# The end of a one-core decoder layer: combining additions of the first row tile ahead of the second's, small sums of squares joined or moved to ScalarE

## The chip, the core and the metric

The kernel runs on one core of a Trainium2 chip. The core has TensorE for matmuls (its results go to PSUM, in banks of 128 x 512 float32), VectorE and ScalarE for elementwise work, GpSimd, and SyncE, which mostly issues DMAs; each works through its own queue of instructions in order and waits on semaphores for the others. SBUF is the working memory of 128 partitions. The metric is the device time of one execution in microseconds, the median of several runs. In the profile's rows PE is TensorE, PEld its weight load, DVE VectorE, ACT ScalarE, POOL GpSimd, SP SyncE; a small q behind a name is that engine's sequencer.

## What is computed

One decoder layer on 256 tokens of width 2048: a normalized input goes through sparse attention and a convolution module side by side, then a gated MLP with a short causal convolution, then a last RMS norm. The change touches only the last line: the residual sum and that norm.

```python
def rms_norm(x, g):
    xf = x.astype(jnp.float32)
    y = xf * lax.rsqrt(jnp.mean(xf * xf, axis=-1, keepdims=True) + NORM_EPS)
    return (y * g.astype(jnp.float32)).astype(x.dtype)
...
        x = x + jnp.concatenate([attn, conv], axis=-1) @ w_out[l]
        h = rms_norm(x, ffn_norm_g[l])
        x = x + conv_glu_ffn(h, w_up[l], ffn_conv_w[l], ffn_conv_b[l], w_down[l])
    return rms_norm(x, final_norm_g)
```

## The kernel before

The 256 tokens are two row tiles of 128 tokens (`t` = 0 and 1), each on the 128 partitions; `x2[:, t]` holds a row tile's 2048 columns of the residual sum, and the tail below adds the MLP's result into it and norms it. Every float32 product is made of three or four matmuls of a high and a low part (`wh`, `wl`, `gh`, `gl`).

The MLP's down projection runs in two halves of 1024 output columns (`h`), 22 chunks of weights each. Many chunks are of the kind "S": a scheme with 7 products in place of 8, whose results stand in banks by name (1 to 8) and have to be combined by additions at the end. In the second half, name 2 is bank 6 and name 3 is bank 7 (row tile 0, its two quarters of 512 columns), name 4 is bank 0 and name 8 is bank 1 (row tile 1); names 1, 5, 6 and 7 are banks 2, 3, 4 and 5. `combine` (L1409) returns the nine steps: ScalarE copies bank 2 to `c`; bank 3 is added to the second quarter of row tile 0 (step 1) and of row tile 1 (step 2); `u` = bank 4 + `c` (step 3); `v` = `u` - bank 5 (step 4); row tile 0 gets + `c` (step 5) and - `u` (step 6); row tile 1 gets + `v` (step 7) and - `v` (step 8).

The last two chunks are of kind "D", plain products, and `last_quad` (L1476) puts them out in six pieces, so that the norm can begin early: for each row tile its third quarter (columns 1024 to 1536) whole, piece 0, in banks 6 and 0, and its last quarter (1536 to 2048) as two pieces of 256 columns, in banks 2 and 4 for row tile 0 and banks 3 and 5 for row tile 1. Those four banks are free only when `combine` has read them.

`last_add` (L1447) adds a piece to `x2` on VectorE; ScalarE squares and sums it into a column of `ss3`. Columns 0 and 1 of `ss3` were filled long before, from the first 1024 columns. `last_root` (L1454) sums the squares of the last piece on VectorE (the custom instruction), starting from the sum of the others, and GpSimd raises it to the power -0.5: the root `r`. `last_scale` (L1465) multiplies by the root, ScalarE for columns of the first half (already multiplied by the weights of the norm) and VectorE for the second half with the weights, and issues the store. The small sums that join the columns of `ss3` are instructions of 128 x 1: `mean_of` (L275) on VectorE, `more` (L1481) on ScalarE.

The order on each engine is the order of the code (the schedule is manual): all of `combine` for both row tiles, then the direct additions of banks 7 and 1 (L1518), then row tile 0's pieces, its small sums and root, then row tile 1. SyncE issues the stores, ScalarE the very last one.

Of the kernel before, what the change touches and what calls it, by code (L numbers as in the profile page):

```python
# [11 lines left out]
F32 = mybir.dt.float32  # L12
F32R = mybir.dt.float32r
AF = mybir.ActivationFunctionType
# [39 lines left out]
def hybrid_trunk(ctx: ExitStack, tc: tile.TileContext, a: dict, out: bass.AP):  # L54
# [220 lines left out]
    def mean_of(pool, parts_, count, acc=EPS):  # L275

        for p_ in parts_:
            ms = pool.tile([P, 1], F32, name="ms", bufs=4)
            nc.vector.tensor_scalar(ms, p_, 1.0 / count, acc, op0=OP.mult, op1=OP.add)
            acc = ms  # L280
        return acc
# [925 lines left out]
    with ExitStack() as fx:  # L1207
# [239 lines left out]
        def last_add(b, t, i):  # L1447
            lo, hi = LAST[i]
            xq = x2[:, t, 1024 + lo:1024 + hi]
            nc.vector.tensor_add(xq, b, xq)  # L1450
            if i < 2:
                nc.scalar.activation(sq3[:, :hi - lo], xq, AF.Square, scale=ROOT, accum_out=ss3[:, t, 2 + i:3 + i])

        def last_root(t, acc):  # L1454
            lo, hi = LAST[2]
            xq = x2[:, t, 1024 + lo:1024 + hi]
            nc.vector.tensor_tensor_reduce(out=sq3[:, 256:], in0=xq, in1=xq, scale=1.0 / D, scalar=acc,
                                           op0=OP.mult, op1=OP.add, accum_out=ss3[:, t, 4:5])
            r = fw.tile([P, 1], F32, name="rstd", bufs=2)
            nc.gpsimd.tensor_tensor(r, ss3[:, t, 4:5], half, op=OP.pow)  # L1460
            return r

        accs = []

        def last_scale(t, r3, lo, hi, whole=True, between=None, queue=nc.sync):  # L1465
            there, here = [v.rearrange("p (a c) -> p a c", a=2)[:, :, lo:hi] for v in (out_rows[:, t], x2[:, t])]
            nc.vector.scalar_tensor_tensor(here[:, 1], here[:, 1], r3, gfin[:, 1024 + lo:1024 + hi],
                                           op0=OP.mult, op1=OP.mult)
            if not whole:
                nc.sync.dma_start(there[:, 1], here[:, 1])  # L1470
                there, here = there[:, :1], here[:, :1]
                accs.append(between())
            nc.scalar.activation(x2[:, t, lo:hi], x2[:, t, lo:hi], AF.Copy, scale=r3)
            queue.dma_start(there, here)

        def last_quad(ws2, g, b0):  # L1476

            def sums(t, parts_, acc=EPS):
                return mean_of(fw, [ss3[:, t, i:i + 1] for i in parts_], 1, acc)

            def more(t, i, acc):  # L1481
                new = fw.tile([P, 1], F32, name="more", bufs=2)
                nc.scalar.activation(new, ss3[:, t, i:i + 1], AF.Identity, bias=acc)
                return new

            for i in range(3):
                last_add(last_products(ws2, g, b0[0], 0, i), 0, i)
            acc = sums(1, range(2))
            r0 = last_root(0, sums(0, range(4)))
            b = last_products(ws2, g, b0[1], 1, 0)  # L1490
            nc.vector.tensor_add(x2[:, 1, 1024:1536], b, x2[:, 1, 1024:1536])
            last_scale(0, r0, 0, 512)
            nc.scalar.activation(sq3, x2[:, 1, 1024:1536], AF.Square, scale=ROOT, accum_out=ss3[:, 1, 2:3])
            last_add(last_products(ws2, g, b0[1], 1, 1), 1, 1)
            last_scale(0, r0, 512, 1024, False, lambda: more(1, 3, sums(1, (2,), acc)))
            last_add(last_products(ws2, g, b0[1], 1, 2), 1, 2)
            r1 = last_root(1, accs.pop())
            for lo, hi in ((0, 256), (256, 512), (512, 1024)):
                last_scale(1, r1, lo, hi, queue=nc.scalar if hi == 1024 else nc.sync)

# [10 lines left out]
        for h in range(2):  # L1511
            nb = dict(zip((2, 3, 4, 8, 1, 5, 6, 7), ring[4 * h:] + ring[:4 * h]))
            for q in range(NQ):
                g = gq.pop(0)
                if h == 1 and q == NQ - 1:
                    run_todo(99)
                    for t in range(2):
                        nc.vector.tensor_add(x2[:, t, 1536:], nb[names[t, 1]], x2[:, t, 1536:])  # L1518
                    ws2 = w_next(), w_next()
                    last_quad(ws2, g, [nb[names[t, 0]] for t in range(2)])  # L1520
                    break
                if prev and q == 0:
                    todo.extend(lambda t=t, n=n, nb=prev: first_add(nb, t, n) for t in range(2) for n in range(2))
                    todo.extend(lambda i=i: first_half(i // 2, i % 2) for i in range(4))
                for j in range(2):
                    p = 2 * q + j
                    down_pair(h, p, g, j, nb)
                    if KINDS[h].rfind("S") == p:
                        todo.extend(combine(h, nb))
            prev = nb  # L1530

# [97 lines left out]
```

## Time and profile before

| what | value |
|---|---|
| median of 3 runs | 1082.1 us (1082.0 to 1082.76) |
| the profiled execution | 1081.91 us |
| its span, first to last instruction | 1080.1 us |
| granted TensorE clock, mean | 0.998 of full |
| TensorE busy | 1070.4 us, 99% of the span |
| VectorE busy | 897.6 us, 83% |
| ScalarE busy | 619.9 us, 57% |
| GpSimd busy | 367.8 us, 34% |
| 1060 to 1066 us: VectorE / ScalarE busy | 5.95 / 0.00 of 6 us |
| 1066 to 1070 us: VectorE / ScalarE busy | 3.60 / 1.27 of 4 us |
| 1070 to 1075 us: TensorE / VectorE / ScalarE busy | 1.93 / 4.06 / 4.03 of 5 us |

The span is 1.8 us shorter than the run's own time, which also has what lies around the first and the last instruction. Times in rows are microseconds from the start of the span. A timeline row is start, duration, engine, line of the code, operation, out<-in, the shape and how many; where several of one line follow each other they are merged (x2, x3) into one duration. What stands in brackets behind a row is how long the engine was idle ahead of it, and what ended that.

### The profile page before, as it was taken

The page shows a single profiled execution, that of the slowest core. Times are in us where ns is not written, and L with a number is a line of the kernel's source. Part 1 is how long each engine was busy: PE and PEld are TensorE (multiplying, and loading weights), DVE is VectorE, ACT ScalarE, POOL GpSimd, SP SyncE. Part 2 cuts the span into 40 slices and gives each one's busy share as a digit, 9 for nine tenths or more (in the row PEclk, how much of TensorE's full clock was granted, in tenths as well). Part 3 has the DMA queues.
Part 4 walks back from the last instruction along what each step waited for, and adds up shares of the span by engine and source line. Part 5 has one row for each costly group of instructions (what it writes and reads, how often), then busy time and mean ns, then how long its engine had stood idle before and what let it go on. Part 6 is the DMA issues. An engine that isn't in the chain of part 4 may idle for free.

```text
span 1080.1 us, 17521 instructions
## 1 busy us (share of the span) xinstructions
PE 1070.4 (99%) x6721; PEld 954.3 (88%) x6721; DVE 897.6 (83%) x1429; ACT 619.9 (57%) x895; POOL 367.8 (34%) x420
## 2 busy tenths in 40 slices
PE   9999999999999999999999999999999999999996
PEld 9999999998788888888888888888888888888886
DVE  6799976777896677878787888878788899999997
ACT  7544456878755555556555555555555556565563
POOL 0888966657100202324233433212121222211220
PEclk9999999999999999999999999999999999999999
DMA  9776757323555878999999999866667699979982
GB/s 353 245 259 257 210 150 240 119 79 118 195 195 199 273 237 244 287 289 282 296 267 304 294 295 299 280 224 224 225 216 276 208 393 352 344 286 345 336 311 98
DMA packets 62016, 272.82 MB, mean 253 GB/s; under 512 B 8187, under 2 KB 11531, under 8 KB 42348
## 3 DMA queue, kind: packets, MB, share of 16 engines
q1 hardware_dynamic: 34748, 199.33, 51.4%
q0 software_dynamic: 23536, 65.29, 22.7%
q10 hardware_dynamic: 3648, 7.08, 1.9%
q8 instruction: 53, 0.87, 0.3%
q14 instruction: 31, 0.25, 0.1%
HBM read 254.87 MB, written 41.18 MB: 274 GB/s over the span
## 4 chain that ended last, share of the span: by engine, by line
PE 96%; DVE 2%; ACT 1%; issue 0%; POOLq 0%; POOL 0%; DVEq 0%; ACTq 0%
PE bank L1355 30%; PE bank L1357 15%; PE bank L253 6%; PE bank L255 6%; PE bank L244 5%; PE bank L246 5%; PE bank L245 5%; PE bank L256 3%; PE bank L254 3%; PE bank L261 3%; PE bank L262 3%; PE bank L263 3%; PE bank L1009 1%; PE bank L986 1%; PE bank L941 1%; DVE wl L211 1%
## 5 line engine op out<-in xcount | busy, mean ns | idle before, releaser
L1355 PE MATMUL bank<-xt,wh 128*128 128x512 f32 x1408 | 488.6, 394 | 0.0
L206 ACT ACTIVATE wh<-wraw 128x1024 fp32r<-128x1024 f32 (+2 forms) x187 | 263.4, 1430 | 279.9 <-issue 113.1
L1357 PE MATMUL bank<-xt,wl 128*128 128x256 f32 x1408 | 390.1, 277 | 0.0
L211 DVE TENSOR_TENSOR wl<-wraw,wh 128x2048 fp32r<-128x2048 f32 (+1 forms) x133 | 254.6, 1919 | 104.9 <-ACT wh L206 104.9
L1355 PEld LDWEIGHTS bank<-xt,wh 128*128 128x128 f32 x1408 | 264.0, 188 | 61.3
L1357 PEld LDWEIGHTS bank<-xt,wl 128*128 128x128 f32 x1408 | 264.2, 188 | 0.0
L244 PE MATMUL bank<-xt,wh 128*128 128x256 f32 x502 | 143.7, 286 | 0.0
L246 PE MATMUL bank<-xt,wl 128*128 128x256 f32 x502 | 142.1, 283 | 0.0
L245 PE MATMUL bank<-xt,wh 128*128 128x256 f32 x502 | 142.0, 283 | 0.0
L211 POOL TENSOR_TENSOR wl<-wraw,wh 128x1024 fp32r<-128x1024 f32 (+1 forms) x54 | 122.6, 2325 | 18.7 <-ACT wh L206 18.7
L128 DVE TENSOR_TENSOR wl<-wraw,wh 128x2048 fp32r<-128x2048 f32 x44 | 100.4, 2285 | 4.6 <-ACT wh L127 4.5
L244 PEld LDWEIGHTS bank<-xt,wh 128*128 128x128 f32 x502 | 96.1, 192 | 1.5 <-issue 0.9
L245 PEld LDWEIGHTS bank<-xt,wh 128*128 128x128 f32 x502 | 96.2, 192 | 0.4
L246 PEld LDWEIGHTS bank<-xt,wl 128*128 128x128 f32 x502 | 96.2, 192 | 0.1
L518 DVE SCALAR_TENSOR_TENSOR bank<-us,cw,bank 128x256 f32<-128x256 f32 x232 | 93.4, 481 | 0.7 <-ACT bank L513 0.3
L1260 POOL DMA_DIRECT2D sum<-in_w_d x84 | 64.5, 846 | 73.2 <-issue 49.2
L127 ACT ACTIVATE wh<-wraw 128x2048 fp32r<-128x2048 f32 x44 | 82.9, 1904 | 7.5 <-PE bank L1355 4.0
L127 ACT ACTIVATE xh<-sums 128x1536 fp32r<-128x1536 f32 x28 | 41.8, 1493 | 78.2 <-DVE sums L156 56.7
L1294 DVE SCALAR_TENSOR_TENSOR yt<-u,fcw,yt 128x255 f32<-128x255 f32 (+1 forms) x176 | 80.9, 480 | 3.1
L1325 POOL DMA_DIRECT2D glf<-glt x22 | 12.9, 586 | 192.3 <-DVE glt L128 136.2
L253 PE MATMUL bank<-wh,gh 128*128 128x512 f32 x167 | 65.6, 393 | 0.0
L255 PE MATMUL bank<-wl,gh 128*128 128x512 f32 x167 | 65.5, 392 | 0.0
(308 smaller groups left out, 1872.0 us busy)
## 6 DMA issues: line engine op xcount, KB each, us to landing
wraw<-in_w_u SPq DMA_DIRECT2D x88, 1024.0 KB, 7.6
wraw<-in_w_t SPq DMA_DIRECT2D x28, 1024.0 KB, 5.1
sum<-in_w_d POOLq DMA_DIRECT2D x84, 256.0 KB, 8.3
wraw<-in_w_d SPq DMA_DIRECT2D x28, 768.0 KB, 7.0
wraw<-in_w_d SPq DMA_DIRECT2D x16, 1024.0 KB, 7.1
gs<-gsf POOLq DMA_DIRECT2D x56, 256.0 KB, 6.3
wraw<-in_w_o SPq DMA_DIRECT2D x13, 1024.0 KB, 4.8
gl<-glf POOLq DMA_DIRECT2D x22, 512.0 KB, 5.4
```

What stands on the lines that cost most here:

```text
L127: nc.scalar.activation(hi, src, AF.Copy)
L128: return lambda: nc.vector.tensor_sub(lo, src, hi.bitcast(F32))
L206: nc.scalar.activation(h[:, sl], raw[:, sl], AF.Copy)
L211: (nc.gpsimd if pooled else nc.vector).tensor_sub(l[:, sl], raw[:, sl], h[:, sl].bitcast(F32))
L244: nc.tensor.matmul(ps, wh, xh, start=first, stop=False)
L245: nc.tensor.matmul(ps, wh, xl, start=False, stop=False)
L246: nc.tensor.matmul(ps, wl, xh, start=False, stop=last)
L253: nc.tensor.matmul(ps, xh, wh, start=first, stop=False)
L255: nc.tensor.matmul(ps, xh, wl, start=False, stop=False)
L518: nc.vector.scalar_tensor_tensor(y[:, j] if last else acc[0], us[:, j, k:k + T], cw[:, j, k:k + 1], acc[0], op0=OP.mult, op1=OP.add)
L1355: nc.tensor.matmul(bk[i], wh[:, k, sl], xt[kt // 4][:, kt % 4].rearrange("p a t -> p (a t)"), start=kt == 0, stop=False)
L1357: nc.tensor.matmul(bk[i][:, :T], wl[:, k, sl], xt_h[kt], start=False, stop=kt == KD - 1)
```

## The change

`last_quad` now receives the nine steps of `combine` and the direct addition as arguments, and places them itself: what row tile 0 needs comes first, row tile 1's additions lie between row tile 0's pieces and behind its sum of squares. Columns 0 and 1 of `ss3` of both row tiles, with the epsilon, are added by one VectorE instruction into `firsts`; the other small sums are made by `more` on ScalarE. In `last_scale` the ScalarE part is written ahead of VectorE's, and where its store is split in two, the half that is stored first is now ScalarE's.

```diff
-        accs = []
...
         def last_scale(t, r3, lo, hi, whole=True, between=None, queue=nc.sync):
             there, here = [v.rearrange("p (a c) -> p a c", a=2)[:, :, lo:hi] for v in (out_rows[:, t], x2[:, t])]
-            nc.vector.scalar_tensor_tensor(here[:, 1], here[:, 1], r3, gfin[:, 1024 + lo:1024 + hi],
-                                           op0=OP.mult, op1=OP.mult)
+            nc.scalar.activation(x2[:, t, lo:hi], x2[:, t, lo:hi], AF.Copy, scale=r3)
             if not whole:
-                nc.sync.dma_start(there[:, 1], here[:, 1])
-                there, here = there[:, :1], here[:, :1]
-                accs.append(between())
-            nc.scalar.activation(x2[:, t, lo:hi], x2[:, t, lo:hi], AF.Copy, scale=r3)
+                nc.sync.dma_start(there[:, 0], here[:, 0])
+                there, here = there[:, 1:], here[:, 1:]
+                between()
+            nc.vector.scalar_tensor_tensor(x2[:, t, 1024 + lo:1024 + hi], x2[:, t, 1024 + lo:1024 + hi], r3,
+                                           gfin[:, 1024 + lo:1024 + hi], op0=OP.mult, op1=OP.mult)
             queue.dma_start(there, here)
...
-            for i in range(3):
-                last_add(last_products(ws2, g, b0[0], 0, i), 0, i)
-            acc = sums(1, range(2))
-            r0 = last_root(0, sums(0, range(4)))
-            b = last_products(ws2, g, b0[1], 1, 0)
-            nc.vector.tensor_add(x2[:, 1, 1024:1536], b, x2[:, 1, 1024:1536])
+            for i in (0, 1, 3, 6):
+                merge[i]()
+            direct(0)
+            merge[5]()
+            firsts = fw.tile([P, 2], F32, name="firsts", bufs=1)
+            nc.vector.scalar_tensor_tensor(firsts, ss3[:, :, 0], EPS, ss3[:, :, 1], op0=OP.add, op1=OP.add)
+            merge[2]()
+            last_add(last_products(ws2, g, b0[0], 0, 0), 0, 0)
+            acc = more(0, 2, firsts[:, :1])
+            merge[4]()
+            last_add(last_products(ws2, g, b0[0], 0, 1), 0, 1)
+            acc = more(0, 3, acc)
+            merge[7]()
+            last_add(last_products(ws2, g, b0[0], 0, 2), 0, 2)
+            r0 = last_root(0, acc)
+            merge[8]()
             last_scale(0, r0, 0, 512)
+
+            def beside():
+                direct(1)
+                b = last_products(ws2, g, b0[1], 1, 0)
+                nc.vector.tensor_add(x2[:, 1, 1024:1536], b, x2[:, 1, 1024:1536])
+
+            last_scale(0, r0, 512, 1024, False, beside)
             nc.scalar.activation(sq3, x2[:, 1, 1024:1536], AF.Square, scale=ROOT, accum_out=ss3[:, 1, 2:3])
+            acc = more(1, 2, firsts[:, 1:])
             last_add(last_products(ws2, g, b0[1], 1, 1), 1, 1)
-            last_scale(0, r0, 512, 1024, False, lambda: more(1, 3, sums(1, (2,), acc)))
+            acc = more(1, 3, acc)
             last_add(last_products(ws2, g, b0[1], 1, 2), 1, 2)
-            r1 = last_root(1, accs.pop())
+            r1 = last_root(1, acc)
...
-                    if KINDS[h].rfind("S") == p:
+                    if h == 0 and KINDS[h].rfind("S") == p:
                         todo.extend(combine(h, nb))
```

TensorE's matmuls keep their number and order. How the other queues change is best seen in the instructions as they stand on each engine (line, operation, out<-in, shape, and what the instruction waits for). The first place is VectorE's queue from its first combining addition to row tile 0's sum of squares; `x2_3709` is the residual sum and `cuv_10666` holds `c`, `u` and `v`. Before:

```order
L1420 TENSOR_TENSOR x2_3709<-bank3_67,x2_3709 128x512 [waits PE_49]
L1420 TENSOR_TENSOR x2_3709<-bank3_67,x2_3709 128x512
L1421 TENSOR_TENSOR cuv_10666<-bank4_68,cuv_10666 128x512 [waits Activation_49]
L1421 TENSOR_TENSOR cuv_10666<-cuv_10666,bank5_69 128x512 [waits DVE_49]
L1422 TENSOR_TENSOR x2_3709<-x2_3709,cuv_10666 128x512 x2
L1423 TENSOR_TENSOR x2_3709<-x2_3709,cuv_10666 128x512 [waits DVE_49]
L1423 TENSOR_TENSOR x2_3709<-x2_3709,cuv_10666 128x512
L1518 TENSOR_TENSOR x2_3709<-bank7_71,x2_3709 128x512 [waits DVE_49]
L1518 TENSOR_TENSOR x2_3709<-bank1_65,x2_3709 128x512 [waits DVE_49]
L1450 TENSOR_TENSOR x2_3709<-bank6_70,x2_3709 128x512 [waits PE_49]
L1450 TENSOR_TENSOR x2_3709<-bank2_66,x2_3709 128x256 [waits DVE_49,PE_49]
L1450 TENSOR_TENSOR x2_3709<-bank4_68,x2_3709 128x256 [waits PE_49]
```

Behind these stood six small sums (L279), then the sum of squares. Of the change, the same place:

```order
L1420 TENSOR_TENSOR x2_3709<-bank3_67,x2_3709 128x512 [waits PE_49]
L1421 TENSOR_TENSOR cuv_10666<-bank4_68,cuv_10666 128x512 [waits Activation_49]
L1422 TENSOR_TENSOR x2_3709<-x2_3709,cuv_10666 128x512 [waits DVE_49]
L1532 TENSOR_TENSOR x2_3709<-bank7_71,x2_3709 128x512 [waits DVE_49]
L1422 TENSOR_TENSOR x2_3709<-x2_3709,cuv_10666 128x512
L1486 SCALAR_TENSOR_TENSOR firsts_10673<-ss3_8766 128x2
L1420 TENSOR_TENSOR x2_3709<-bank3_67,x2_3709 128x512
L1450 TENSOR_TENSOR x2_3709<-bank6_70,x2_3709 128x512 [waits DVE_49,PE_49]
L1421 TENSOR_TENSOR cuv_10666<-cuv_10666,bank5_69 128x512
L1450 TENSOR_TENSOR x2_3709<-bank2_66,x2_3709 128x256 [waits PE_49]
L1423 TENSOR_TENSOR x2_3709<-x2_3709,cuv_10666 128x512 [waits DVE_49]
L1450 TENSOR_TENSOR x2_3709<-bank4_68,x2_3709 128x256 [waits PE_49]
```

Row tile 0's pieces (L1450) moved from rows 10 to 12 to rows 8, 10 and 12, row tile 1's last step (the second L1423, less `v`) and its direct addition (bank 1) moved behind row tile 0's last piece, and the small sums are gone but for `firsts`.

The second place is what follows on VectorE, from row tile 0's sum of squares (L1457) to row tile 1's. Before:

```order
L1457 ISA sq3_8767,ss3_8766<-x2_3709,ms_10732 128x256 [waits DVE_49]
L1457 ISA ss3_8766 128x1
L1491 TENSOR_TENSOR x2_3709<-bank0_64,x2_3709 128x512 [waits PE_49]
L1467 SCALAR_TENSOR_TENSOR x2_3709<-x2_3709,rstd_10735,gfin_4200 128x512 [waits Pool_49]
L1450 TENSOR_TENSOR x2_3709<-bank3_67,x2_3709 128x256 [waits PE_49]
L1467 SCALAR_TENSOR_TENSOR x2_3709<-x2_3709,rstd_10735,gfin_4200 128x512 [waits DVE_49]
L279 TENSOR_SCALAR ms_10773<-ss3_8766,ms_10724 128x1 [waits Activation_49]
L1450 TENSOR_TENSOR x2_3709<-bank5_69,x2_3709 128x256 [waits PE_49]
L1457 ISA sq3_8767,ss3_8766<-x2_3709,more_10775 128x256 [waits DVE_49,Activation_49]
```

Of the change (the second row of both pieces reads the accumulator):

```order
L1457 ISA sq3_8767,ss3_8766<-x2_3709,more_10710 128x256 [waits DVE_49,Activation_49]
L1457 ISA ss3_8766 128x1
L1423 TENSOR_TENSOR x2_3709<-x2_3709,cuv_10666 128x512
L1470 SCALAR_TENSOR_TENSOR x2_3709<-x2_3709,rstd_10727,gfin_4200 128x512 [waits Pool_49]
L1532 TENSOR_TENSOR x2_3709<-bank1_65,x2_3709 128x512 [waits DVE_49]
L1502 TENSOR_TENSOR x2_3709<-bank0_64,x2_3709 128x512 [waits PE_49]
L1470 SCALAR_TENSOR_TENSOR x2_3709<-x2_3709,rstd_10727,gfin_4200 128x512
L1450 TENSOR_TENSOR x2_3709<-bank3_67,x2_3709 128x256 [waits DVE_49,PE_49]
L1450 TENSOR_TENSOR x2_3709<-bank5_69,x2_3709 128x256 [waits PE_49]
L1457 ISA sq3_8767,ss3_8766<-x2_3709,more_10771 128x256 [waits DVE_49,Activation_49]
```

The root runs on GpSimd between the sum of squares and the first scaling (L1467 before, L1470 in the change): beside it VectorE had the addition out of bank 0, and now has the last subtraction of `v`. Both scalings of row tile 0 now stand ahead of row tile 1's second piece (bank 3).

The third place is ScalarE's queue from row tile 0's first square to the last small sum. Before:

```order
L1452 ACTIVATE sq3_8767,ss3_8766<-x2_3709 128x512 [waits DVE_49]
L1452 ACTIVATE sq3_8767,ss3_8766<-x2_3709 128x256 [waits DVE_49,Activation_49]
L1473 ACTIVATE x2_3709<-x2_3709,rstd_10735 128x512 [waits Pool_49]
L1493 ACTIVATE sq3_8767,ss3_8766<-x2_3709 128x512 [waits DVE_49,Activation_49]
L1452 ACTIVATE sq3_8767,ss3_8766<-x2_3709 128x256 [waits DVE_49,Activation_49]
L1483 ACTIVATE more_10775<-ss3_8766,ms_10773 128x1 [waits DVE_49,Activation_49]
```

Of the change:

```order
L1452 ACTIVATE sq3_8767,ss3_8766<-x2_3709 128x512 [waits DVE_49]
L1478 ACTIVATE more_10693<-ss3_8766,firsts_10673 128x1 [waits Activation_49]
L1452 ACTIVATE sq3_8767,ss3_8766<-x2_3709 128x256 [waits DVE_49]
L1478 ACTIVATE more_10710<-ss3_8766,more_10693 128x1 [waits Activation_49]
L1465 ACTIVATE x2_3709<-x2_3709,rstd_10727 128x512 [waits Pool_49]
L1465 ACTIVATE x2_3709<-x2_3709,rstd_10727 128x512
L1505 ACTIVATE sq3_8767,ss3_8766<-x2_3709 128x512 [waits DVE_49]
L1478 ACTIVATE more_10755<-ss3_8766,firsts_10673 128x1 [waits Activation_49]
L1452 ACTIVATE sq3_8767,ss3_8766<-x2_3709 128x256 [waits DVE_49]
L1478 ACTIVATE more_10771<-ss3_8766,more_10755 128x1 [waits Activation_49]
```

Three `more` are added, and the second scaling of row tile 0 moved from behind row tile 1's small sum to ahead of its first square.

More of the change, by code (lines that the diff above doesn't have):

```diff
@@ L1461, in last_root, with last_quad @@
             return r
-        accs = []
         def last_scale(t, r3, lo, hi, whole=True, between=None, queue=nc.sync):
             there, here = [v.rearrange("p (a c) -> p a c", a=2)[:, :, lo:hi] for v in (out_rows[:, t], x2[:, t])]
-            nc.vector.scalar_tensor_tensor(here[:, 1], here[:, 1], r3, gfin[:, 1024 + lo:1024 + hi],
-                                           op0=OP.mult, op1=OP.mult)
+            nc.scalar.activation(x2[:, t, lo:hi], x2[:, t, lo:hi], AF.Copy, scale=r3)
             if not whole:
-                nc.sync.dma_start(there[:, 1], here[:, 1])
-                there, here = there[:, :1], here[:, :1]
-                accs.append(between())
-            nc.scalar.activation(x2[:, t, lo:hi], x2[:, t, lo:hi], AF.Copy, scale=r3)
+                nc.sync.dma_start(there[:, 0], here[:, 0])
[3 more added lines that the diff above has]
+                                           gfin[:, 1024 + lo:1024 + hi], op0=OP.mult, op1=OP.mult)
             queue.dma_start(there, here)
-        def last_quad(ws2, g, b0):
-            def sums(t, parts_, acc=EPS):
-                return mean_of(fw, [ss3[:, t, i:i + 1] for i in parts_], 1, acc)
+        def last_quad(ws2, g, b0, merge, direct):
             def more(t, i, acc):
@@ L1516, in hybrid_trunk @@
                     run_todo(99)
-                    for t in range(2):
-                        nc.vector.tensor_add(x2[:, t, 1536:], nb[names[t, 1]], x2[:, t, 1536:])
                     ws2 = w_next(), w_next()
-                    last_quad(ws2, g, [nb[names[t, 0]] for t in range(2)])
+                    last_quad(ws2, g, [nb[names[t, 0]] for t in range(2)], combine(h, nb),
+                              lambda t: nc.vector.tensor_add(x2[:, t, 1536:], nb[names[t, 1]], x2[:, t, 1536:]))
                     break
```

## Prediction

> **What bounds the kernel now.** I read the chain of waits first, then the timeline of its last 25 us, then the DMA traffic behind the last instruction. On the page the chain is nearly all matmuls, so outside the tail this change has nothing to act on.
>
> ```profile
> PE 96%; DVE 2%; ACT 1%; issue 0%; POOLq 0%; POOL 0%; DVEq 0%; ACTq 0%
> ```
>
> Told in order of time, the tail of that chain seems to run through exactly what is changed: VectorE's additions, the first row tile's root on GpSimd, then the second root.
>
> ```profile
> 1066.15 1.34 DVE x L1450 x3
> ...
> 1069.37 0.56 POOL rstd L1460
> 1069.93 3.14 issue
> ```
>
> The row to stop at is the 3.14 us of "issue": between the two roots the chain shows nothing that was waited for. It went back along GpSimd's own queue to the root before, and GpSimd only stood there. The timeline shows what ended last (start, duration, engine, line, out<-in).
>
> ```profile
> 1071.63 0.21 DVE L279 TENSOR_SCALAR ms<-ss,ms 128x1 f32<-128x1 f32 x1
> 1071.64 0.28 PE L263 MATMUL bank<-wh,gl 128*128 128x256 f32 x1
> ...
> 1071.93 0.29 ACT L1483 ACTIVATE more<-ss,ms 128x1 f32<-128x1 f32 x1
> 1071.96 0.42 DVE L1450 TENSOR_TENSOR x<-bank,x 128x256 f32<-128x256 f32 x1
> ...
> 1072.53 0.48 DVE L1457 CUSTOM_DVE_ANT_0 sq<-x,more 128x256 bf16<-128x256 f32 x1
> ...
> 1073.10 0.55 POOL L1460 TENSOR_TENSOR rstd<-ss,half 128x1 f32<-128x1 f32 x1 [3.18 <-DVE ss L1457]
> 1073.69 1.54 DVE L1467 SCALAR_TENSOR_TENSOR x<-x,rstd,gfin 128x256 f32<-128x256 f32 x3 [0.67 <-POOL rstd L1460]
> 1073.69 1.52 ACT L1473 ACTIVATE x<-x,rstd 128x256 f32<-128x256 f32 x3 [0.86 <-POOL rstd L1460]
> 1075.32 0.64 ACTq L1474 DMA_DIRECT2D out<-x  x1
> ```
>
> The last matmul of the program ends at 1071.64 + 0.28 = 1071.92, and 0.04 later the last addition starts. **That addition waits for TensorE.** From there on everything is serial: addition, sum of squares, root, three scalings, stores. Of the 1080.1 us span, 8.1 lie behind 1071.96. The sum of squares also needs `more` from ScalarE, which was there at 1071.93 + 0.29 = 1072.22, before the addition ended at 1072.38. The wait that stands alone ahead of the sum of squares passed at 1072.4, so the addition was late and `more` was not, with 0.16 us to spare.
>
> ```profile
> L1457 DVEq EVENT_SEMAPHORE  x1: 21/21/21, 1072.4 to 1072.4; - x1
> ```
>
> Last, the stores (stretches; the last two columns are the DMA share and GB/s):
>
> ```profile
> 1075.00:1075.50 0.50, 0.00 (x0) 0.00 (x0) 0.24 (x1) 0.21 (x1) 0.00 (x0) 0.50 0.12 43
> 1075.50:1076.00 0.50, 0.00 (x0) 0.00 (x0) 0.00 (x0) 0.00 (x0) 0.00 (x0) 0.50 1.01 336
> ...
> 1077.50:1078.00 0.50, 0.00 (x0) 0.00 (x0) 0.00 (x0) 0.00 (x0) 0.00 (x0) 0.50 1.03 385
> ```
>
> By about 1075.0 the first row tile's stores have drained: the traffic almost stops (43 GB/s), then the second tile's begin. The first tile does not delay the second.
>
> **The change part by part.** TensorE issues the same matmuls in the same order. Its pieces of the last product end at the last row of each (start plus duration):
>
> ```profile
> 1063.08 0.40 PE L263 MATMUL bank<-wh,gl 128*128 128x512 f32 x1
> ...
> 1064.61 0.28 PE L263 MATMUL bank<-wh,gl 128*128 128x256 f32 x1
> ...
> 1066.03 0.28 PE L263 MATMUL bank<-wh,gl 128*128 128x256 f32 x1
> ...
> 1068.70 0.39 PE L263 MATMUL bank<-wh,gl 128*128 128x512 f32 x1
> ...
> 1070.23 0.28 PE L263 MATMUL bank<-wh,gl 128*128 128x256 f32 x1
> ```
>
> That is 1063.48, 1064.89 and 1066.31 for the first row tile, 1069.09, 1070.51 and (above) 1071.92 for the second. TensorE gets one wait more, ahead of the second tile's middle piece, for the addition of bank 3. That piece starts right behind the 1068.70 row; in my schedule the addition is done at 1064.1. Cost nothing, with over 4 us of cover. Bank 5, needed at about 1070.4, is read by 1065.4.
>
> VectorE's steps come from these rows:
>
> ```profile
> 1060.02 1.29 DVE L1420 TENSOR_TENSOR x<-bank,x 128x512 f32<-128x512 f32 x2 [0.62 <-PE bank L263]
> 1061.22 0.68 DVE L1421 TENSOR_TENSOR cuv<-bank,cuv 128x512 f32<-128x512 f32 x1
> 1061.94 0.69 DVE L1421 TENSOR_TENSOR cuv<-cuv,bank 128x512 f32<-128x512 f32 x1
> ...
> 1066.15 1.34 DVE L1450 TENSOR_TENSOR x<-bank,x 128x512 f32<-128x512 f32 x3
> 1067.41 0.14 DVE L279 TENSOR_SCALAR ms<-ss 128x1 f32<-128x1 f32 x1
> ...
> 1068.79 0.48 DVE L1457 CUSTOM_DVE_ANT_0 sq<-x,ms 128x256 bf16<-128x256 f32 x1
> ...
> 1069.20 0.69 DVE L1491 TENSOR_TENSOR x<-bank,x 128x512 f32<-128x512 f32 x1
> 1069.96 0.75 DVE L1467 SCALAR_TENSOR_TENSOR x<-x,rstd,gfin 128x512 f32<-128x512 f32 x1
> 1070.63 0.42 DVE L1450 TENSOR_TENSOR x<-bank,x 128x256 f32<-128x256 f32 x1
> ```
>
> From start to start: 0.60 for an addition of 512 columns (two in 1.20), 0.72 where the next needs its result (1061.22 to 1061.94), 0.33 for 256 columns ((1067.41 - 1066.15 - 0.60) / 2), 0.41 behind the sum of squares, 0.67 for a scaling. The addition ahead of a sum of squares starts 0.57 before it (1071.96 to 1072.53).
>
> *First row tile.* From the same 1060.02: bank 3 into it 1060.02, `u` 1060.62, less `u` 1061.34, bank 7 1062.06, plus `c` 1062.66, `firsts` 1063.26 (0.2, an estimate from the 0.14 row), bank 3 into the second tile 1063.46, piece 0 1064.06 (its matmuls ended 1063.48, so VectorE and not TensorE sets it), `v` 1064.66, piece 1 1065.26, plus `v` 1065.59, then piece 2 at 1066.35, just behind its matmuls at 1066.31. Sum of squares 1066.35 + 0.57 = **1066.92 against 1068.79: 1.87 us earlier**. The gain comes from the second tile's four additions pushed behind or between, and from six small sums on VectorE (1067.41 to 1068.79 in all, 1.38) that go away.
>
> The small sums become four additions on ScalarE. Its rows:
>
> ```profile
> 1066.86 0.63 ACT L1452 ACTIVATE sq<-x 128x512 bf16<-128x512 f32 x1 [9.05 <-DVE x L1450]
> 1067.40 0.19 ACT L1452 ACTIVATION_READ_ACCUMULATOR sq<-x 128x1 f32 x1
> ...
> 1071.33 0.42 ACT L1452 ACTIVATE sq<-x 128x256 bf16<-128x256 f32 x1
> 1071.65 0.19 ACT L1452 ACTIVATION_READ_ACCUMULATOR sq<-x 128x1 f32 x1
> ...
> 1072.13 0.71 ACT L1473 ACTIVATE x<-x,rstd 128x512 f32<-128x512 f32 x1
> ```
>
> A square starts 0.03 behind the addition's end (1066.15 + 0.68 against 1066.86); its accumulator is read 0.54 later (0.32 at 256 columns); `more` starts 0.28 behind that and holds ScalarE for 0.20 (1071.93 to 1072.13). First tile: square 1064.77, read 1065.31, `more` 1065.59, square 1065.79, read 1066.11, `more` 1066.39 to 1066.69. VectorE wants it when its addition ends, 1066.77. Hidden, by only 0.08.
>
> *The first root* starts 0.57 behind the sum of squares (1072.53 to 1073.10), so at 1067.49. But beside it VectorE now takes `v` off the second tile, an addition with both inputs in SBUF; before, an addition out of PSUM stood there. The start of the kernel shows what that does to a root:
>
> ```profile
> 28.47 1.46 POOL L399 TENSOR_TENSOR rc<-ms,half 128x1 f32<-128x1 f32 x1 [27.18 <-DVE ms L279]
> 28.30 1.22 DVE L401 CUSTOM_DVE_ANT_0 sqd<-xr 128x1024 bf16<-128x1024 f32 x1
> ```
>
> This root took 1.46 us, not 0.55, beside a VectorE pass whose two inputs are both in SBUF, and ended 29.93, 0.41 behind that pass. The Trainium skill says so too: in "SBUF — State Buffer", section "SBUF: two separate sides", GpSimd and a VectorE instruction with two SBUF inputs hold one pair of ports as an exclusive lock for a whole instruction, and the trace agrees (1.46 against 0.55). It speaks against the change: by it the first scaling starts 0.38 us later than without it, which the sum below takes from the rows. The addition runs 1067.33 to 1068.01, the root ends 1068.42, and the scaling starts at **1068.46** against 1069.96. With an undisturbed root it would be 1068.08, and the end the same.
>
> *Second row tile.* VectorE: scaling 1068.46, bank 1 at 1069.13, piece 0 at 1069.73, scaling 1070.33, piece 1 at 1071.00 (before 1070.63), piece 2 at **1071.96: TensorE's end, as before**. So the gain of 1.5 us at the root is an idle stretch from 1071.42 to 1071.96. ScalarE: two scalings back to back from 1068.46 to 1069.8, square 1070.45, read 1070.97, `more` 1071.25, square 1071.45, read 1071.77, `more` 1072.05, done 1072.35. The addition it meets ends at 1072.38; what was 0.16 to spare is 0.03. Cost nothing, but the cover is almost gone, and each 0.1 us beyond is paid in full.
>
> *Stores.* SP's first store and the first of its last three belong to the first row tile:
>
> ```profile
> 1070.79 0.65 SPq L1474 DMA_DIRECT2D out<-x  x1
> ...
> 1072.86 2.60 SPq L1474 DMA_DIRECT2D out<-x  x3
> ```
>
> The first goes from 1070.79 to about 1069.3, behind the scaling of 1068.46, the third from 1072.86 to about 1071.15, behind that of 1070.33, into a DMA queue that stood empty. The second tile's stay where they are, since they wait for the second root. Worth nothing while the gap at 1075.0 is there. The second root has no VectorE work beside it, before or after.
>
> **Sum:** behind 1071.96 nothing is removed or added, so the change is 0. Span 1080.1, run 1081.91 as profiled, and by the median of the runs shown, 0.19 above the profiled one, **1082.1 us**.
>
> **The rivals.**
>
> *The early root carries to the end.* The chain of waits runs through the first root, and it comes 1.5 us earlier (1.87 at the sum of squares). If my reading of the 1071.96 wait were wrong (ends of matmuls are modelled), up to 1.87 would reach the end: 1080.2 us. For it: the chain. Against it: 0.04 us between the last matmul and the addition, and the step ahead of the addition had ended at 1071.63 + 0.21 = 1071.84, so VectorE was free. A smaller form: if the 0.15 between the addition's end and the sum of squares was a wait for `more`, and if the last stores, now behind a longer pause, went at the later 385 GB/s rather than 336 in their first 0.5 us, 0.2 to 0.3 is won: 1081.8.
>
> *`more` becomes the late link.* Place: VectorE takes its queue in order, so its first scaling holds back piece 1 behind it, that holds ScalarE's square and `more`, and `more` the last sum of squares. Point: the first scaling later than about 1068.5. Price: all that it is later. If the root ran its full 0.56 only after the addition, the scaling would come at 1068.60 and cost 0.1; one more hitch on ScalarE of the size of a `more` step (0.28 + 0.20) adds 0.5: 1082.2 to 1082.7, slower. For it: my 0.03 of slack. To pass 2.2 us the scaling would have to come at 1070.7, later than the 1069.96 of before.
>
> *The change does not do what it says:* the order of the instructions shows that it does.
>
> **How the numbers follow.** A measurement of this kernel can tell about 0.2%, 2.2 us, from no change. No change in the end, within 0.3 us: 0.78. Early root carries through in part or whole, 1080.2 to 1081.8: 0.10, nearly all of it still within 0.2%, since 1.87 is less than 2.2. Late `more`, 1082.2 to 1082.7: 0.08. Something that these rows do not show, of over 2 us: 0.02 on each side. Faster 0.03 (0.02 and a little of the first rival), same 0.95, slower 0.02. The three runs of before spread by 0.76 us. Low end: 1082.1 less 0.3 for the smaller gains, less that spread, 1081.0; high end: 1082.1 plus 0.2 for a slightly late `more`, plus the spread, 1083.1.
>
> **What would show it.** In the profile after: the first sum of squares near 1066.9, the first root longer than 0.8 us, the first scaling near 1068.5, `more` ending close to 1072.35, the last addition still at 1071.96 directly behind TensorE, the last sum of squares at 1072.5. I am wrong if the last addition starts earlier than TensorE's end allows, if the last sum of squares starts clearly later than 0.57 behind it (then `more` is late), or if TensorE shows a gap behind 1060.

## The result: 12 us slower, and none of it in the tail

| | before | change |
|---|---|---|
| median of 4 runs each, us | 1082.17 (1082.0 to 1082.76) | 1094.34 (1094.24 to 1094.39) |
| span of the profiled execution, us | 1080.1 | 1092.5 |
| granted clock | 0.998 | 0.999 |
| TensorE busy | 1070.4 | 1082.3 |

The ratio is 1.0112, with a 95% interval of 1.0099 to 1.0124. The forecast was 1082.1, with a range up to 1083.1.

First the tail, the part that was changed. Rows of the change's timeline (start, duration, engine, line, out<-in; in brackets the idle time ahead and what ended it):

```profile
1072.44 0.69 DVE L1420 TENSOR_TENSOR x<-bank,x 128x512 f32<-128x512 f32 x1 [0.71 <-PE bank L263]
...
1079.36 0.48 DVE L1457 CUSTOM_DVE_ANT_0 sq<-x,more 128x256 bf16<-128x256 f32 x1
1079.76 0.08 DVE L1457 DVE_READ_ACCUMULATOR2_ANT ss<- 128x1 f32 x1
1079.76 0.69 DVE L1423 TENSOR_TENSOR x<-x,cuv 128x512 f32<-128x512 f32 x1
1079.93 0.94 POOL L1460 TENSOR_TENSOR rstd<-ss,half 128x1 f32<-128x1 f32 x1 [15.65 <-DVE ss L1457]
1080.91 0.75 DVE L1470 SCALAR_TENSOR_TENSOR x<-x,rstd,gfin 128x512 f32<-128x512 f32 x1 [0.46 <-POOL rstd L1460]
...
1084.09 0.28 PE L263 MATMUL bank<-wh,gl 128*128 128x256 f32 x1
...
1084.40 0.42 DVE L1450 TENSOR_TENSOR x<-bank,x 128x256 f32<-128x256 f32 x1 [0.55 <-PE bank L263]
1084.43 0.29 ACT L1478 ACTIVATE more<-ss,more 128x1 f32<-128x1 f32 x1
1084.97 0.48 DVE L1457 CUSTOM_DVE_ANT_0 sq<-x,more 128x256 bf16<-128x256 f32 x1
```

The last matmul ends at 1084.09 + 0.28 = 1084.37, and the last addition starts at 1084.40. Before, that addition started at 1071.96. So the whole tail stands 1084.40 - 1071.96 = 12.44 us later, and from there to the end of the span it takes 1092.5 - 1084.4 = 8.1 us, as before. At the first row, the first addition, it is 1072.44 - 1060.02 = 12.42. The loss lies ahead of the tail.

The groups by line show it (busy us, mean ns of one). Before:

```profile
L1355 PE MATMUL bank<-xt,wh 128*128 128x512 f32 x1408 | 488.6, 394 | 0.0
L1357 PE MATMUL bank<-xt,wl 128*128 128x256 f32 x1408 | 390.1, 277 | 0.0
L253 PE MATMUL bank<-wh,gh 128*128 128x512 f32 x167 | 65.6, 393 | 0.0
```

And of the change:

```profile
L1355 PE MATMUL bank<-xt,wh 128*128 128x512 f32 x1408 | 497.8, 399 | 0.0
L1357 PE MATMUL bank<-xt,wl 128*128 128x256 f32 x1408 | 395.5, 281 | 0.0
L253 PE MATMUL bank<-wh,gh 128*128 128x512 f32 x167 | 66.2, 397 | 0.0
```

The same 1408 matmuls of the up projection (L1355 and L1357), hundreds of microseconds ahead of the changed code, are each 4 to 5 ns longer, with no idle time ahead of them in either kernel. Since these durations overlap and their ends are modelled, it is better to count starts. The windows of TensorE (stretch; busy us and in brackets the matmuls; granted clock; DMA share; GB/s) of before:

```profile
400.00:500.00 100.00, 100.00 (x579) 1.00 0.92 265
700.00:800.00 100.00, 100.00 (x579) 1.00 0.66 229
900.00:1000.00 100.00, 100.00 (x570) 1.00 0.91 331
```

And of the change:

```profile
400.00:500.00 100.00, 100.00 (x567) 1.00 0.89 260
700.00:800.00 100.00, 100.00 (x567) 1.00 0.66 225
900.00:1000.00 100.00, 100.00 (x562) 1.00 0.90 324
```

TensorE is busy without a gap at a granted clock of 1.00 in both, and does 567 matmuls in 100 us where it did 579. The counts are the same whether the DMA share is 0.9 (400 to 500) or 0.66 (700 to 800), so traffic doesn't explain it. Set against each other matmul by matmul (both kernels issue the same 6721, in the same order), the change lags by 0.3 us at 357 us and by 0.42 at 374; from there by another 0.333 us for each 100 matmuls, to 9.50 us at 846 us, the end of the up projection; then more slowly to 12.44 at the end. What stands at 366.6 us in the kernel before (timeline):

```profile
366.48 0.28 PE L1357 MATMUL bank<-xt,wl 128*128 128x256 f32 x1
366.60 0.60 PE L1203 MATMUL bank<-dg,ones 128*128 128x128 f32 x4
366.96 0.47 PE L1355 MATMUL bank<-xt,wh 128*128 128x512 f32 x1
```

Four small matmuls, which read the tile `dg2` (`dg` in the row), interrupt the stream of alternating matmuls of 512 and 256 columns. The times from start to start around them, in ns, worked out from the starts in the trace (theirs between the bars):

```
before  ... 232 118 241 120 236 113 232 118 241 119 |108 110 112 31| 313 113 232 118 230 113 232 118 231 112 233 117 ...
change  ... 233 117 241 120 236 113 233 117 241 119 |109 110 111 31| 316 118 235 114 232 118 241 120 235 114 232 118 ...
```

**There are two rhythms.** Up to these matmuls both kernels run 232, 118, 241, 120, 236, 113: some 707 ns for four matmuls. Behind them the kernel before falls into a quicker one, 693.3 ns for four, and keeps it to the end of the stage, for 479 us; the change goes on in the slow one, 706.7. That is 13.3 / 4 = 3.33 ns for each of the 2766 matmuls that follow in that stage: 9.2 us.

What differs between two programs that issue the same matmuls? Their operands' addresses in SBUF. The diff takes small tiles out of the pool `fw` (four `ms` go, one `firsts` comes, each in a slot of 32 bytes), so this pool is 96 bytes shorter, and every tile allocated behind it, in the pools `fu` (up projection) and `fd` (down projection), begins 96 bytes lower. From the two compiled programs, in bytes within a partition:

```
tile                              before    change
dg2 (moving operand of L1203)     190656    190560
gs0, gs1 (gate sums, down)        208704, 188224   208608, 188128
wh4, wl4 (every 4th weights, down) 212800, 220992  212704, 220896
xt, wh, wl, gh, gl                unmoved
```

All tiles of these two pools were at multiples of 64 and are now 32 beyond one. Of those that moved, TensorE reads only the ones listed. The operands of the slow up projection itself (`xt`, `wh`, `wl`) are not among them.

### The profile page after: what moved, and what is told of

The parts are those of the page before. It is cut to its first block, busy times and chain, and to the rows that moved or that the text cites. A ratio compares the mean times of both kernels' runs of the same rounds, so it can differ in the third digit from the quotient of the medians.

```text
span 1092.5 us, 17514 instructions
## 1 busy us (share of the span) xinstructions
PE 1082.3 (99%) x6721; PEld 958.9 (88%) x6721; DVE 896.7 (82%) x1423; ACT 620.7 (57%) x898; POOL 367.8 (34%) x420
## 4 chain that ended last, share of the span: by engine, by line
PE 96%; DVE 2%; ACT 1%; issue 1%; DMA 1%; SPq 0%; POOL 0%; POOLq 0%; DVEq 0%; ACTq 0%
PE bank L1355 30%; PE bank L1357 15%; PE bank L255 6%; PE bank L253 6%; PE bank L244 5%; PE bank L246 5%; PE bank L245 5%; PE bank L256 3%; PE bank L254 3%; PE bank L261 3%; PE bank L263 3%; PE bank L262 3%; PE bank L1009 1%; PE bank L986 1%; PE bank L941 1%
## 5 line engine op out<-in xcount | busy, mean ns | idle before, releaser
L1355 PE MATMUL bank<-xt,wh 128*128 128x512 f32 x1408 | 497.8, 399 | 0.0
L1357 PE MATMUL bank<-xt,wl 128*128 128x256 f32 x1408 | 395.5, 281 | 0.0
L1355 PEld LDWEIGHTS bank<-xt,wh 128*128 128x128 f32 x1408 | 264.6, 188 | 65.8
L1357 PEld LDWEIGHTS bank<-xt,wl 128*128 128x128 f32 x1408 | 266.0, 189 | 0.0
L246 PE MATMUL bank<-xt,wl 128*128 128x256 f32 x502 | 142.1, 283 | 0.0
```

What stands on the lines that cost most here:

```text
L246: nc.tensor.matmul(ps, wl, xh, start=False, stop=last)
L1355: nc.tensor.matmul(bk[i], wh[:, k, sl], xt[kt // 4][:, kt % 4].rearrange("p a t -> p (a t)"), start=kt == 0, stop=False)
L1357: nc.tensor.matmul(bk[i][:, :T], wl[:, k, sl], xt_h[kt], start=False, stop=kt == KD - 1)
```

## The experiments

**The theory and its rivals.** Theory: the order in the tail is worth nothing, as forecast, and the 12 us come from the addresses. Rival: something else in the changed program (its instructions, its semaphores) makes TensorE slower. The first run keeps the whole change, and only widens one small tile so that all others lie where they were:

```diff
-            firsts = fw.tile([P, 2], F32, name="firsts", bufs=1)
+            firsts = fw.tile([P, 32], F32, name="firsts", bufs=1)[:, :2]
```

> All of the change, with the tile firsts widened to 128 bytes, so that every tile behind it in SBUF stands at the address that it had before (the change had moved them by 96 bytes). Address theory: the 12.4 us that TensorE lost between 357 and 1070 us are gone, 1081.5 to 1082.7 us, and the rest is the effect of the new order at the end alone, which the prediction put at 0. Order theory (the new instructions themselves make it slower): 1094.

Measured: 1082.16 us against 1082.05, ratio 1.0001 (0.9993 to 1.001). So **the addresses are the whole loss**, and the new order by itself is worth nothing that can be measured.

The second goes the other way: the kernel before with its moved tiles 32 bytes higher, hence 32 beyond a multiple of 64, too.

```diff
-                new = fw.tile([P, 1], F32, name="more", bufs=2)
+                new = fw.tile([P, 1], F32, name="more", bufs=3)
```

> The kernel before with one more buffer for the small tile more, nothing else: all tiles behind it move by 32 bytes, from a multiple of 64 to 32 beyond one. Address theory: slower by 9 to 13 us, 1091 to 1095, with the loss in the same stages as in the change. Order theory: 1082.

Measured: 1083.41 against 1082.05, ratio 1.0013 (1.0004 to 1.0023). The expectation missed: the up projection keeps 693 ns, and the 1.4 us all come in the down projection. "32 beyond a multiple of 64" is not what makes the up projection slow. This splits the change's loss: some 9 us behind the L1203 matmuls, some 3 us in the down projection.

The runs that follow, up to the last one, are single executions. Those of the kernel before lie between 1081.55 and 1082.76 us, so a difference below 1 us in the total says little by itself; the lag behind the kernel before, matmul by matmul within one stage, is steadier (in the up projection it stays within 0.02 us where the rhythm is the same).

**Which tile does it in the up projection?** Next `dg2` was moved by itself, by taking it out of a wider tile at an offset (the tiles behind it in its pool, none of which TensorE reads, move up by as much as the tile is wider). In the kernel before, to 190688:

```diff
-                dg.append(fu.tile([P, 2, P], F32, name="dg2", bufs=1))
+                wide = fu.tile([P, 2 * P + 16], F32, name="dg2", bufs=1)
+                dg.append(wide[:, 8:8 + 2 * P].rearrange("p (a b) -> p a b", a=2))
```

> The kernel before with only the tile dg2 (the diagonal that four matmuls at about 367 us read, after which the long even stream of the up projection begins) 32 bytes beyond a multiple of 64; every other tile stays at a multiple of 64. Rhythm theory (TensorE falls into one of two lasting rhythms at the restart behind those four matmuls): the up projection loses about 9 us as in the change, 1090 to 1095. Contention theory (VectorE's and ScalarE's tiles at 32 beyond a multiple of 64 slow TensorE's reads all the time): 1082.

Measured: 1082.23 us, nothing: what the rival had forecast, not the rhythm theory, whose guess was again that 32 beyond a multiple of 64 is what counts. The same edit in the change puts `dg2` at 190592, a multiple of 64; the other moved tiles stay 32 beyond one:

> The change with only dg2 put back at a multiple of 64, all other moved tiles still 32 beyond one. Rhythm theory: the up projection is as fast as before, and the loss is at most the 3 us that the down projection had: 1082 to 1085.5. Contention theory: 1094.

Measured: 1084.89 us. The up projection is back at 693 ns per four, though VectorE's and ScalarE's tiles still lie 32 beyond a multiple of 64, so here the contention theory, with its 1094, falls. 2.7 us are left, all in the down projection. But the edit also makes the tile larger, and pushes the ones behind it. So a control: the change with the wider tile, `dg2` at offset 0 and thus where the change has it:

```diff
-                dg.append(wide[:, 8:8 + 2 * P].rearrange("p (a b) -> p a b", a=2))
+                dg.append(wide[:, 0:0 + 2 * P].rearrange("p (a b) -> p a b", a=2))
```

> The changed kernel with the tile dg2 16 columns wider: dg2 itself stays at its new address (190560), the tiles behind it in the same pool lie 64 bytes further, those of the last pool as in the changed kernel. Address theory (the address of dg2 alone makes TensorE leave the four matmuls that read it in the slow rhythm): slow as the changed kernel, 1094 to 1095 us, 707 ns per four matmuls behind 367 us. Rival (the restart is a matter of chance or of the other tiles): 693 ns per four matmuls in the up projection, and 1084 to 1086 us, as the run in which dg2 lay at a multiple of 64.

Measured: 1093.85, slow. The last two runs differ in nothing but where `dg2` begins in the same wider tile, by 32 bytes. Their windows, at 190592:

```profile
400.00:500.00 100.00, 100.00 (x579) 1.00 0.90 266
```

and at 190560:

```profile
400.00:500.00 100.00, 100.00 (x568) 1.00 0.87 260
```

And, in the kernel before, `dg2` at 191072, which like the 190560 of the change is 96 beyond a multiple of 512 (the tile wider by 128 columns, offset 104, so the tiles behind it in its pool lie 512 bytes higher):

> The kernel before with dg2 alone at 191072, which has the same remainder by 512 as the 190560 of the changed kernel; all other tiles at multiples of 64. If the address of dg2 within 512 bytes decides: slow rhythm in the up projection, 707 ns per four matmuls, 1091 to 1093 us. Rival (it needs the other moved tiles too, or decides by something else): 693 ns and 1082 us, as in the run with dg2 32 beyond a multiple of 64.

Measured: 1091.43 against 1082.53. Its windows:

```profile
400.00:500.00 100.00, 100.00 (x569) 1.00 0.88 259
700.00:800.00 100.00, 100.00 (x569) 1.00 0.65 224
900.00:1000.00 100.00, 100.00 (x570) 1.00 0.92 327
```

569 matmuls in 100 us of the up projection (707 ns for four, from start to start) where the kernel before has 579; 570 in the down projection, as before. Its lag grows from 0.1 us at 357 us to 9.3 at the end of the up projection, and is 9.5 at the end. **One tile, read by four matmuls that take 0.6 us, makes the next 479 us slower by 9 us**, in a kernel that has the old order and, but for those 512 bytes, the old addresses. Slow was `dg2` at 96 beyond a multiple of 512, at two addresses; fast were 128, 192 and 224.

**An address that slows matmuls, or a rhythm that the restart picks?** The up projection doesn't read `dg2`, so the slow matmuls are the same ones at the same addresses. First I only moved the L1203 matmuls, one pair of up projection matmuls later:

```diff
-                   (0, 12): lambda: (x2_evac(14), x2_evac(15)), (1, 8): x2_spread}
+                   (0, 12): lambda: (x2_evac(14), x2_evac(15)), (1, 9): x2_spread}
```

> The changed kernel with the same addresses, and only the four small matmuls that read dg2 put behind another group of the up projection. Rhythm theory (TensorE holds a rhythm until it is interrupted, and the interruption picks the next one): the rhythm behind the four matmuls may come out as 693 ns per four, then 1084 to 1086 us; if it is slow again from the new place, 1094 us plus or minus 0.5. Rival (the addresses make each matmul of the up projection slower, whatever comes before): 1094 us, with the slow rhythm in all of the up projection in any case.

Measured: 1094.27, slow as the change. Both theories allow that. So the next run has ten more interruptions, at known places: behind every fourth group of the up projection the same kind of small products, of the ones with `dg2` or with the identity, two or one of them, into a bank that the next group overwrites. Nothing reads these extra products.

```diff
+        breaks = {(4, 1, 8): ("dg2", 2), (8, 1, 8): ("ident", 2), (12, 1, 8): ("dg2", 1), (16, 1, 8): ("ident", 1),
+                  (20, 1, 9): ("dg2", 2), (24, 1, 3): ("ident", 2), (28, 1, 8): ("dg2", 2), (32, 1, 8): ("ident", 2),
+                  (36, 1, 5): ("ident", 1), (40, 1, 12): ("dg2", 1)}
...
+                        if (2 * m + part, kh, n) in breaks:
+                            what, calls = breaks[2 * m + part, kh, n]
+                            for t in range(calls):
+                                nc.tensor.matmul(UP_BANKS[2 * ((2 * m + part + 1) % 4)][:, t * P:(t + 1) * P], ones,
+                                                 dg[0][:, t] if what == "dg2" else ident, start=True, stop=True)
```

The change with these:

> The changed kernel, same addresses, with ten extra interruptions of the up projection, four groups of columns apart: one or two products of the ones with dg2 or with the identity (whose results nothing reads), each some 0.25 to 0.5 us. Rhythm theory (a stretch of TensorE keeps its rhythm until it is interrupted, and a shift of a few ns at the restart picks the next one): behind some of the ten the rhythm changes to 693 ns per four matmuls and stays there until the next interruption, so TensorE's delay against the kernel before grows by 0.333 us per 100 matmuls in some stretches and not in others. Rival (the addresses make each matmul slower): 707 ns in all stretches, and 1094 us plus 3 to 5 for the extra matmuls.

Measured: 1092.38 us. **With ten interruptions of extra work the changed kernel is 2 us faster than without.** And the kernel before with the same ten, not one address changed:

> The kernel before, with its own addresses, and the same ten interruptions. Rhythm theory: behind some of them TensorE falls into 707 ns per four matmuls and stays there until the next, with not one address changed. Rival (addresses alone): 693 ns in all stretches, 1082 us plus 3 to 5 for the extra matmuls.

Measured: 1088.48 against 1082.27. Here are its windows, each of 35 us between two interruptions:

```profile
375.00:410.00 35.00, 35.00 (x204) 1.00 0.75 239
420.00:455.00 35.00, 35.00 (x204) 1.00 0.92 270
465.00:500.00 35.00, 35.00 (x204) 1.00 0.97 275
510.00:545.00 35.00, 35.00 (x200) 1.00 0.98 286
555.00:590.00 35.00, 35.00 (x200) 1.00 0.94 275
600.00:635.00 35.00, 35.00 (x204) 1.00 0.99 286
```

The count drops from 204 to 200 at the interruption of 501 us, stays there past that of 547, and is back at 204 behind that of 593: TensorE falls into the slow rhythm and leaves it again, each time at an interruption and never between two. Here is what each picked, from the starts in the trace, in ns per four matmuls up to the next interruption (times of the run with the change):

```
interruption at    367   412   458   503   548   593   637   683   728   772   819
reads              dg2   dg2  ident  dg2 ident   dg2 ident   dg2 ident ident   dg2
change, ten more   707   707   693   693   707   707   693   693   693   693   707
before, ten more   693   693   693   707   707   693   693   693   693   693   707
```

Both rhythms come in both kernels, and reading `dg2` at its new address is followed by the fast one too (503, 683). So the rival falls that the addresses make each matmul slow, whatever comes before.

The table is no row of chance draws, though. Take the interruptions by two products (those at 503, 548, 772 and 819 us have one). Two products of the ones with the identity, or with `dg2` at its old address, are followed by 693 ns every time, ten of ten, whatever the rhythm ahead of them. Two products with `dg2` at its new address leave the rhythm as it was: 707 behind 707 at 367, 412 and 593, 693 behind 693 at 683. The other runs fit: ahead of the L1203 matmuls the rhythm is 707 in all of them, and behind them it is 693 with `dg2` at 128, 192 or 224 beyond a multiple of 512, and 707 at 96. Behind a single product either rhythm followed, even with the same tile and the same rhythm ahead (in the change, `dg2` at 503 and at 819).

The sums agree. The extra products cost some 3.6 us in either kernel (the time lost at each interruption, added up). In the change, the fast stretches of 458 to 548 and 637 to 819 us hold some 1560 matmuls, worth 1560 x 3.33 ns = 5.2 us: net -1.6, measured -2.0 against the change's 1094.34. In the kernel before, 712 matmuls run slow, 2.4 us, and 3.6 + 2.4 = 6.0 against the measured 6.2.

**The down projection.** The change with only the last pool put back, by a tile of 96 bytes at its start:

> The changed kernel with a pad of 96 bytes first in the last pool: what TensorE reads and what is written in the down projection lies at the addresses of before, dg2 as in the changed kernel. Theory of two parts (up projection by the restart behind dg2, down projection by the addresses of its operands): up projection slow, plus 9.1 us, down projection as before, so 1091 to 1092 us. Rival (one cause, a rhythm that lasts from the up projection to the end): down projection loses about 3 us as well, 1094 us.

Measured: 1092.44. The up projection is slow as expected. In the down projection the steady loss is gone: of the 1.2 us that it still loses, 1.0 come at one place, at 949 to 954 us, where TensorE waited for the DMA of a tile of gate sums:

```profile
952.20 0.47 PE L253 MATMUL bank<-xh,gs 128*128 128x512 f32 x1 [0.58 <-DMA gs<-gsf]
```

Why that DMA was late, in the one execution that was profiled, stays open. Then the change with `dg2` at 190592, and in the last pool a pad ahead of `wh4` and `wl4` alone, so that these two lie at their old addresses and `gs0` and `gs1` don't:

```diff
+            late_pool[0].tile([P, 24], F32, name="pad", bufs=1)
             h = late_pool[0].tile([P, CW], F32R, name="wh4", bufs=1)
```

> The changed kernel with dg2 at a multiple of 64 (as in the run of that alone, which lost 2.7 us in the down projection), and a pad that puts the two split weight tiles of the last pool back to their old addresses, while the two tiles of summed gates (gs0, gs1) stay 32 bytes beyond a multiple of 64. If the weights, which TensorE streams 512 columns at a time, cost the 2.7 us: down projection as before, 1082 to 1082.6 us. If the sums of gates, which it loads as weights of 128 columns, cost it: 1084.5 to 1085 us.

Measured: 1083.22. Neither expectation: the down projection loses 1.4 us where it lost 2.7 (2.9 in the change itself), so the addresses of the weights are worth about half. The other half is left to the gate sums or to the pool's tiles that TensorE doesn't read (`wraw4`, `sums` and `cuv`, still 32 beyond a multiple of 64 in this run); no run separates them. Matmuls in 100 us of that stage, in this kernel:

```profile
900.00:1000.00 100.00, 100.00 (x567) 1.00 0.90 328
```

With `dg2` alone mended (1084.89 us) it is

```profile
900.00:1000.00 100.00, 100.00 (x562) 1.00 0.91 329
```

and before, above, 570.

Nor is it shown that TensorE reads the moved tiles more slowly. Set against the kernel before from start to start, the change loses 1.57 of its 2.9 us at the 697 matmuls of this stage (of 1296) that read no moved tile, 2.3 ns each; the 385 that read moved gate sums and unmoved weights lose 2.3 ns each, too. So here as well matmuls with unmoved operands take longer.

**A version with the new order and without the loss.** One more buffer for `more` in the change, the same one word as in the second run, shifts everything behind to multiples of 64 again, 64 bytes lower than before:

> The changed kernel with three buffers for `more` in place of two, one word: every tile behind lies 64 bytes lower than before, at multiples of 64 again, not at the addresses of before. If 64 byte steps are what matters for the down projection, and dg2 at remainder 128 by 512 gives the fast rhythm (as in the run with dg2 there): 1082 us, ratio 0.999 to 1.001. Rival (only the very addresses of before are fast): 1085 to 1094 us.

Measured: 1082.56 against 1082.27, ratio 1.0004 (0.9995 to 1.0014). The very addresses of before aren't needed; the down projection still loses 0.5 us. No version that was run beats the kernel before by more than a measurement can tell.

## Why the prediction was wrong

**The steps of the tail held.** Less the shift of the first addition (1072.44 - 1060.02 = 12.42), the measured times stand beside the forecast ones:

| step | forecast | measured; the same less 12.42 |
|---|---|---|
| first sum of squares | 1066.92 | 1079.36; 1066.94 |
| first root, duration | 0.93 | 0.94 |
| first scaling | 1068.46 | 1080.91; 1068.49 |
| last `more` done | 1072.35 | 1084.72; 1072.30 |
| last addition | 1071.96, at TensorE's end | 1084.40; 1071.98, which is 0.03 behind TensorE's end |

The first root ended at 1079.93 + 0.94 = 1080.87, 0.42 behind the end of VectorE's subtraction beside it (1079.76 + 0.69), as the forecast took it from the root of L399; the second root, alone, took 0.55. The rule that the forecast cited from the Trainium skill ("SBUF — State Buffer", section "SBUF: two separate sides": one pair of ports held for a whole instruction) fits this trace again, and cost nothing here either. `more` was done 0.10 us ahead of the addition's end (1084.82), not 0.03. (In the forecast's steps of ScalarE, 1070.45 + 0.54 is 1070.99 and not 1070.97, which changes nothing.) That all this is worth 0 was right: with the old addresses the ratio is 1.0001.

**The step that failed** stands in the forecast's first lines: "outside the tail this change has nothing to act on", and again in "TensorE issues the same matmuls in the same order", for which its sum has no term. The second is true, and that TensorE's time stays the same doesn't follow: outside the tail the change has its allocations to act on. It removed 96 bytes from a pool that lies ahead of two others, and so moved operands of matmuls in stages that it doesn't touch: 9.2 us in the up projection, in the slow rhythm behind the four matmuls that read `dg2`, and 2.9 us in the down projection. The forecast looked at what the diff removes in instructions, not at what it removes in bytes. It gave 0.02 to "something that these rows do not show, of over 2 us" on the slower side, and named no mechanism for it; its range ended at 1083.1, and 1094.34 lies 11.2 us beyond.

**The test that it set itself was the wrong one, too**: "if TensorE shows a gap behind 1060". There is no gap. TensorE was 99% busy in both kernels, and a stage that is 2% slower looks the same in busy shares. The mean durations of the matmuls and their count in a stretch showed it.

**Could it have been seen?** Half of it. In the trace of before, the up projection is interrupted three times at its start: behind four small matmuls at 357.6 us it runs 116, 230, 117, 230 ns (693 for four), behind four at 360.8 us 241, 120, 236, 113, 232, 118 (707), and behind those of 366.6 us 693 again. So that this stage has two rhythms, and can change them at an interruption, was there to read, and so were the moved addresses, in the program. Which address leaves which rhythm was not. A rival "the moved tiles change the rhythm" with a price between 0 and 9 us could have been set up; a range that reached to it would still have ended some 2 us short, by the down projection.

**What stays open.** Why TensorE has two lasting rhythms here, and what holds it in one, no run shows. Nor how the address of `dg2` acts: the step behind the L1203 matmuls was 313 to 315 ns where the fast rhythm followed and 312 to 316 where the slow one did, so it doesn't tell, and that a shift of a few ns decides stays argued. The remainder of 96 by 512 is two addresses of five tried. For the down projection it is shown that the addresses in the last pool cost the time, those of `wh4` and `wl4` about half of it, and that multiples of 64 save nearly all of it; not which other tiles cost, and not by which mechanism.

## What to carry to other kernels

A tile that is removed or added moves every tile allocated behind it, so before a change is judged, compare the operand addresses of both programs, and pad the freed bytes where an untouched stage reads from what moved. When the time changes in a stage that the diff doesn't touch, count instructions in equal windows (busy shares hide a slower rhythm), and repeat the change with the old addresses before believing anything of its order. A difference of one per cent in a stream of like matmuls can be a rhythm that one interruption left behind: interrupt the stream at several places before you call it a property of the matmuls.

## What the runs showed of the hardware that I had not expected

- A stream of alternating 512 and 256 column matmuls, the same code at the same addresses, ran for up to 479 us at 693 or at 707 ns per four, and changed only where a few other matmuls interrupted it, in either direction: at four of ten added interruptions in the change, at three of ten in the kernel before.
- Interruptions by two small products of the ones left 693 ns behind them in every case where the other operand was the identity, or `dg2` at 128, 192 or 224 beyond a multiple of 512; where it was `dg2` at 96 beyond one, the rhythm stayed what it was (707 each time but one).
- With the tiles of the last pool 32 bytes beyond a multiple of 64 the down projection took 1.4 us (moved up by 32 bytes) to 2.9 us (down by 96) longer; at multiples of 64, but 64 bytes lower than before, 0.5.
- Extra work can shorten the time: ten interruptions of 3.6 us in all made the changed kernel 2.0 us faster.
